# A decoder trunk on one core: column sums of the second norm spread among large products, a hand-made engine order through the up projection's fourth pair, two weight splits moved

## The chip, the cores and the metric

The kernel runs on one core of a Trainium2 chip. The metric is the device time of one execution in microseconds (us), of which three were taken before the change: 944.78, 944.92 and 948.59, median 944.92. In the text PE is the matrix engine and PEld its weight loads, DVE the vector engine, ACT the scalar engine, POOL the GpSimd engine, SP the queue that issues the DMAs. A time such as 271.10 is counted from the start of the profiled span.

## What is computed

One decoder layer of 1024 tokens and width 1024: a sliding-window attention, then a squared-ReLU MLP of 4096 hidden units, each behind an RMS norm, and a final norm.

```
u = rms_norm(h, attn_norm);  h = h + swa_mixer(u, w_qkv, sinks, w_o)
u = rms_norm(h, mlp_norm)
a = relu(u @ w_up);          h = h + (a * a) @ w_down
out = rms_norm(h, final_norm)
```

The change touches the second norm (that ahead of the MLP), and the first four of the sixteen groups of the up projection.

## The kernel before

Everything is held transposed: feature rows on the 128 partitions, tokens along the free axis, in two halves `hf` of 512 tokens. A float32 product is made of three fast products: each operand is split into a high part (a cast on ACT) and the low rest (a subtraction on DVE), and `mm3` or `mm3b` add high·high, high·low and low·high into one PSUM bank. One such matmul of 128 x 512 is called a large matmul here, and a product of the up projection is 12 of them.

**The second norm.** The second half of the attention's output projection makes 16 blocks, `oblock(m, hf)`: eight feature blocks m for tokens 0 to 511, then eight for the rest, 12 large matmuls each. Behind each block `oadd` adds it to the residual `h[m]` on DVE, and `square` squares it on ACT into a tile `sq2_m_hf`. Squares 1 to 5 are added onto square 0, one to four on POOL and the fifth on DVE; squares 6 and 7 stay apart. So three tiles hold what is left to sum, and `stat_sum` does it on PE with a vector of ones: `colsum` issues four matmuls with one output column for each tile, 12 in one row. Each is float32 and shows as two matmul records. Then come the root (`rstd`, ACT and small DVE operations) and a diagonal tile `dg` (`diag`, DVE), and `stat_bcast` multiplies it with ones (`n2b` in the trace), which brings the scale of each token to all partitions. `first_half` and `second_half` scale with it.

For tokens 0 to 511 the row of 12 stands behind block (0, 1), and `stat_bcast` behind block (1, 1). For the others the row stands behind the ninth matmul of the up projection's first product, and `stat_bcast` behind the ninth of its second.

**The up projection.** It is Strassen's: `up_mms(n, p)` is product n (1 to 7) of group p (0 to 15), and `up_evac` reads its bank. Products 1, 6, 7, 4 of a group accumulate in one bank of tag X (the copy out behind each must be done before the next may accumulate), product 2 uses Z, 5 and 3 one bank of Y. X has three banks, Y two, Z one. `c11`, `c22`, `c21` and `c12` are its four results, and seven stores per group go to a buffer in DRAM (`hid`). The weight combinations of a group are made from two loads of 512 KB (`wup[p, 0]`, `wup[p, 1]`) with four POOL operations, `up_sums`, and then split. In the rows `sa` and `sb` are the sums, `ws`, `wb`, `wt` and `wa` their splits (`_h`, `_l`).

**What sets the order.** PE always runs in the order in which the code issues (`pe.ordered`). From the second half of the output projection on, DVE, ACT and POOL do so too (`e.ordered = True`), until behind product (6, 2), where it is switched off. Where it is off, a scheduler sets the order of each engine when the kernel is built; each engine then runs its list strictly in that order, and waits at an instruction whose inputs are not ready. SP is one such list too.

Of the kernel before, what the change touches and what calls it, by code (L numbers as in the profile page):

```python
# [10 lines left out]
ALU = mybir.AluOpType  # L11
# [3 lines left out]
P = 128  # L15
# [7 lines left out]
NG = DFF // (2 * P)  # L23
# [39 lines left out]
def trunk(tc, xT, gains, wqkv, wo, wup, wdn, bias_d, sinks_d, ident_d, mask_d, outT):  # L63
# [73 lines left out]
    def colsum(ps, sq, n, first, last):  # L137
        for b in range(n):
            mm(ps[:, b:b + 1], sq[:, b * P:(b + 1) * P], ones[:, 0:1], first and b == 0, last and b == n - 1,
               skip_group_check=True)  # L140

    def rstd(ps, n, name):
        st = const.tile([P, 4, NB], F32, tag="st", name=f"{name}_st", bufs=3)
        var, y0, b_, y = (st[:, i, 0:n] for i in range(4))
        s.activation(y, ps[:, 0:n], AF.Sqrt, bias=eps, scale=1.0 / DM)
        v.tensor_scalar(var, ps[:, 0:n], 1.0 / DM, EPS, op0=ALU.mult, op1=ALU.add)
        v.reciprocal(y0, y)
        v.tensor_tensor(b_, y0, y0, op=ALU.mult)
# [453 lines left out]
    def split1(src, alloc, name):  # L602

        t = two(alloc(F32R, name))
        s.copy(t[:, 0], src)
        v.tensor_tensor(t[:, 1], src, t[:, 0].bitcast(F32), op=ALU.subtract)
        return t[:, 0], t[:, 1]

    def split2(src, alloc, name):

        hi, lo = two(alloc(F32R, f"{name}_h")), two(alloc(F32R, f"{name}_l"))
        s.copy(hi, src)
        v.tensor_tensor(lo, src, hi.bitcast(F32), op=ALU.subtract)
        return [(hi[:, i], lo[:, i]) for i in range(2)]
# [11 lines left out]
    hid = [[dram.tile([P, 2, 512], F32, name=f"hid{i}_{gg}") for gg in range(NG // 2)] for i in range(7)]  # L626
    stat = {}

    def stat_sum(hf):
        ps = bank("Y", f"n2s{hf}")  # L630
        parts = stat.pop(("sq", hf))
        for i, sq in enumerate(parts):
            colsum(ps, sq, 4, i == 0, i == len(parts) - 1)
        rn2 = rstd(ps, 4, f"n2_{hf}")
        dg = sqtile(f"dg2_{hf}")
        diag(rn2, 0, 4, dg)
        stat["dg", hf] = dg
# [6 lines left out]
    def square(m, hf):  # L644
        sl = HALVES[hf]
        sq = sqtile(f"sq2_{m}_{hf}")
        s.activation(sq, h[m][:, sl], AF.Square)
        parts = stat.setdefault(("sq", hf), [])
        if m in (0, 6, 7):
            parts.append(sq)  # L650
        else:
            (g if m < 5 else v).tensor_tensor(parts[0], parts[0], sq, op=ALU.add)

    x1, x2, XP = [], [], {}
    def scaled(out, i, hf, rb):
# [45 lines left out]
    def b22_split(i):  # L701
        XP["b22", i] = split1(h[2 * i + 1][:, HALVES[1]], atile if i else ktile, f"xc{i}")
# [65 lines left out]
    def up_mms(n, p, hooks={}):  # L768
        wn, xn = TERM[n]
        key = {1: "X", 6: "X", 7: "X", 4: "X", 2: "Z", 5: "Y", 3: "Y"}[n]  # L770
        first, last = n in (1, 2, 5), n in (4, 2, 3)
        if first:
            PS[key, p] = bank("mm" if n == 1 and p == 3 else key, f"u{key}{p}")
        for i in range(4):
            mm3b(PS[key, p], WU[wn, p], XP[xn, i], i, first and i == 0, last and i == 3)
            if i in hooks:
                hooks[i]()
# [15 lines left out]
    def c11_relu(p):  # L793
        c11 = OUT["a", p][:, 0]
        s.activation(c11, c11, AF.Relu)
        s.activation(c11, c11, AF.Square)
        store(2, p, c11)
# [64 lines left out]
    def oblock(m, hf):  # L862
        ps = bank(obanks[(hf * KT + m) % 5], f"o1_{m}_{hf}")
        for kk in range(4):
            mm3(ps, wsl(ws[m // 2], (m % 2) * 4 + kk), o_t[4 + kk], HALVES[hf], kk == 0, kk == 3)
        return ps
# [8 lines left out]
        e.ordered = True  # L875
    rb = None
    for m in range(KT):
        ps = oblock(m, 1)
        if m == 1:
            rb = stat_bcast(0)  # L880
        if 2 <= m < 5:
            LO[m - 1] = first_half(m - 1, rb)
        if 2 <= m < 6:
            XP["b11", m - 2], XP["b21", m - 2] = LO[m - 2]()
        if m == 6:
            WU["s2", 0], WU["s1", 0] = LO["ws0"]()
# [91 lines left out]
    for p in (2, 3):
        c11_relu(p)
    WU["a22", 2] = split1(u2[1][:, 1], walloc, "wb2")  # L980
    WU["s3", 2], WU["s4", 2] = split2(u2[0], walloc, "wt2")
    EARLY = 4
    order = [(7, 0), (7, 1), (4, 0), (3, 0), (5, 2), (4, 1), (6, 3), (3, 1), (7, 2), (5, 3), (4, 2), (3, 2),
             (7, 3), (1, 4), (4, 3), (2, 4), (3, 3)]
    for p in range(EARLY, NG):
        nxt = p + 1
        order += [(6, p), (5, p), (7, p)]
        order += ([(1, nxt)] if nxt < NG else []) + [(4, p)] + ([(2, nxt)] if nxt < NG else []) + [(3, p)]
    ready = 3
    for n, p in order:  # L990
        if (n, p) == (7, 1) or (n == 6 and p >= EARLY - 1):

            while ready <= min(max(p + 1, 3), NG - 1):
                raw = up_first(ready, walloc) if ready >= EARLY else None
                up_sums(ready, raw, temp)
                up_splits(ready)
                ready += 1
# [182 lines left out]
```

## Time and profile before

| | |
|---|---|
| median of three runs | 944.92 us |
| the profiled execution | 945.41 us |
| its span, first to last instruction | 943.7 us |
| PE in the chain that ended last | 88% of the span |
| PE waiting between 397 and 625 us | 0.7 us, once |
| mean granted clock of PE | 0.987 |

The chain of work that ended last is PE for 88% of the span. From 397 us to the end of the up projection PE waits once, for 0.7 us. So its waits lie in the first stage, around the second norm, in the first four groups of the up projection and in the final norm. PE's matmul records overlap (a 512-column one shows about 390 ns, while the next starts 226 ns later), so the distance of two starts is what counts.

### The profile page before, as it was taken

The numbers are of one execution on the slowest core, as the hardware profiler recorded it, in microseconds if no ns is written. First come the engines' busy times: TensorE is split into PE (matmuls) and PEld (weight loads), VectorE is DVE, ScalarE is ACT, GpSimd is POOL, SyncE is SP. The second block draws the span as 40 slices with busy tenths as digits, with TensorE's granted clock in tenths as the row PEclk, the third lists the DMA queues.
The fourth block names the chain that finished last, engine by engine and source line by source line (L and its number), as shares of the span: only waits on it lengthen the run. The fifth ranks groups of instructions, "written<-read, shape, count | busy, mean of one in ns | idle before, by whom it ended". The sixth has DMA issues, their size and how long they took to land.

```text
span 943.7 us, 12589 instructions
## 1 busy us (share of the span) xinstructions
PE 917.3 (97%) x4500; PEld 769.9 (82%) x4500; DVE 689.2 (73%) x952; ACT 445.7 (47%) x846; POOL 297.2 (31%) x258
## 2 busy tenths in 40 slices
PE   7999999999989998999999999999999999999996
PEld 6778888888878776888888888878888888888995
DVE  6779988999838886766575656565968785567964
ACT  8578878877534363433433333333333333445510
POOL 5116656566365015455435544110000000040200
PEclk9999999999999999999999999999999999999998
DMA  8200100501353024543454334799898988347622
GB/s 306 69 23 28 52 29 13 201 29 46 119 173 133 33 82 175 189 168 135 144 170 165 134 135 170 273 314 367 302 350 313 351 305 321 109 157 270 264 90 89
DMA packets 57325, 160.35 MB, mean 170 GB/s; under 512 B 6448, under 2 KB 10288, under 8 KB 57264
## 3 DMA queue, kind: packets, MB, share of 16 engines
q1 hardware_dynamic: 57264, 159.57, 47.6%
q8 instruction: 35, 0.57, 0.3%
q14 instruction: 26, 0.21, 0.1%
HBM read 121.79 MB, written 37.75 MB: 169 GB/s over the span
## 4 chain that ended last, share of the span: by engine, by line
PE 88%; DVE 6%; ACT 2%; issue 2%; DMA 1%; POOL 1%; SPq 0%; DVEq 0%; ACTq 0%
PE d L41 33%; PE uX L41 16%; PE f L41 12%; PE uY L41 9%; PE o L41 5%; PE uZ L41 4%; PE pv L41 3%; PE S L41 3%; PE pt L41 1%; DVE xl L41 1%; DMA xr<-xT 1%; PE n2s L41 1%; DVE oa L41 1%; DMA hid<-od 1%; DVE t L41 1%
## 5 line engine op out<-in xcount | busy, mean ns | idle before, releaser
L41 PE MATMUL d<-dx_h,dw_h 128*128 128x512 f32 (+1 forms) x512 | 186.5, 364 | 1.0 <-DVE hr L41 1.0
L41 PE MATMUL d<-dx_l,dw_h 128*128 128x512 f32 (+1 forms) x512 | 185.6, 362 | 0.0
L41 PE MATMUL d<-dx_h,dw_l 128*128 128x512 f32 (+1 forms) x512 | 185.6, 362 | 0.0
L41 PEld LDWEIGHTS d<-dx_h,dw_h 128*128 128x128 f32 x512 | 96.6, 189 | 16.5 <-DVE hr L41 1.4
L41 PEld LDWEIGHTS d<-dx_l,dw_h 128*128 128x128 f32 x512 | 96.6, 189 | 15.4 <-issue 0.2
L41 PEld LDWEIGHTS d<-dx_h,dw_l 128*128 128x128 f32 x512 | 96.6, 189 | 15.0
L41 ACT CAST dx_h<-hr 128x1024 fp32r<-128x1024 f32 x56 | 58.5, 1051 | 57.3 <-DVE dx_l L41 22.3
L41 DVE TENSOR_TENSOR dx_l<-hr,dx_h 128x1024 fp32r<-128x1024 f32 x56 | 71.6, 1285 | 17.6 <-ACT dx_h L41 17.5
L41 ACT CAST dw_h<-wf 128x1024 fp32r<-128x1024 f32 x40 | 41.9, 1052 | 89.6 <-PE d L41 70.7
L41 POOL TENSOR_TENSOR ssq3a<-ssq3a,sq_a 128x512 f32<-128x512 f32 x7 | 12.5, 1789 | 211.1 <-ACT sq_a L41 210.8
L41 DVE TENSOR_TENSOR dw_l<-wf,dw_h 128x1024 fp32r<-128x1024 f32 x40 | 48.6, 1220 | 28.1 <-ACT dw_h L41 27.9
L41 POOL TENSOR_TENSOR t<-t,sm 128x512 f32<-128x512 f32 x32 | 33.3, 1042 | 102.8 <-DVE sm L41 102.8
L41 DVE TENSOR_TENSOR wf<-wd,we 128x1024 f32<-128x1024 f32 x40 | 49.6, 1247 | 18.2 <-DMA we<-wdn 11.2
L41 ACT ACTIVATE t<-t,sm 128x129 f32<-128x129 f32 x128 | 50.5, 397 | 10.9 <-DVE sm L41 10.4
L41 PE MATMUL f<-xh,w_h 128*128 128x512 f32 x128 | 53.7, 420 | 0.0
L41 PE MATMUL f<-xl,w_h 128*128 128x512 f32 x128 | 50.9, 397 | 0.0
L41 PE MATMUL f<-xh,w_l 128*128 128x512 f32 x128 | 50.7, 396 | 0.0
L41 POOL TENSOR_TENSOR ob<-ob,oa 128x512 f32<-128x512 f32 x16 | 20.7, 1291 | 78.4 <-DVE ob L41 78.4
L41 PE MATMUL uX<-xu_h,wb 128*128 128x512 f32 x128 | 42.3, 391 | 2.4 <-ACT oa L41 2.4
L41 POOL TENSOR_TENSOR oc<-oc,oa 128x512 f32<-128x512 f32 x16 | 21.0, 1315 | 73.8 <-DVE oc L41 73.8
L41 ACT COPY oa<-uX 128x512 f32<-128x512 f32 x32 | 18.7, 587 | 49.9 <-PE uX L41 49.9
L41 POOL TENSOR_SCALAR_AFFINE_SELECT cur<-hl 128x1024 fp32r<-128x1024 f32 x32 | 39.5, 1235 | 2.0 <-DVE hl L41 2.0
(351 smaller groups left out, 2406.4 us busy)
## 6 DMA issues: line engine op xcount, KB each, us to landing
wd<-wdn SPq DMA_DIRECT2D x56, 512.0 KB, 5.7
hr<-hid SPq DMA_DIRECT2D x56, 512.0 KB, 4.8
we<-wdn SPq DMA_DIRECT2D x40, 512.0 KB, 7.0
hid<-oa SPq DMA_DIRECT2D x32, 256.0 KB, 2.4
hid<-oc SPq DMA_DIRECT2D x32, 256.0 KB, 2.3
hid<-ob SPq DMA_DIRECT2D x32, 256.0 KB, 2.5
w_r<-wqkv SPq DMA_DIRECT2D x8, 512.0 KB, 3.7
h<-xT SPq DMA_DIRECT2D x8, 512.0 KB, 6.3
```

The costliest lines, as they stand in the source:

```text
L41: ins = method(*args, **kw)
```

## The change

Three things are moved; the arithmetic is the same.

1. *Column sums.* `stat_part` no longer issues the one-column matmuls in a row, but puts them in a list `tiny`, and `mm` issues one behind each large matmul while the list holds any. Those of tokens 0 to 511 go among the 12 matmuls of block (0, 1), the first behind its first matmul; those of tile 0 of the other tokens go among the first four matmuls of block (7, 1), and the other eight among the first eight of the up projection's first product. All five additions of squares are on POOL now.
2. *Splits.* The two splits `a22` of groups 0 and 1 (`wb` in the rows) go from ahead of the loops to behind blocks (3, 1) and (4, 1); the loads of group 2 (`u2`) move from behind block (0, 1) to behind block (4, 1).
3. *Order by hand.* The switch to the scheduler's order comes later, behind product (7, 3). Ahead of it the work of groups 2 and 3 is written out, with `c22_sum` and `d1_sum` for parts of `up_evac`. PE's products are in another order too: (4, 1) is ahead of (5, 2), (3, 1) and (7, 2) ahead of (6, 3), and (4, 2) ahead of (5, 3).

```diff
     def mm(out, lhsT, rhs, start, stop, **kw):
         pe.matmul(out, lhsT=lhsT, rhs=rhs, start=start, stop=stop, **kw)
+        if tiny:
+            tiny.pop(0)()
...
+    def stat_part(hf, i, n=3):
+
+        if i == 0:
+            stat["ps", hf] = bank("Y", f"n2s{hf}")
+        ps, sq = stat["ps", hf], stat["sq", hf][i]
+        for b in range(4):
+            tiny.append(lambda b=b: pe.matmul(
+                ps[:, b:b + 1], lhsT=sq[:, b * P:(b + 1) * P], rhs=ones[:, 0:1], start=i == 0 and b == 0,
+                stop=i == n - 1 and b == 3, skip_group_check=True))
+
     def stat_sum(hf):
-        ps = bank("Y", f"n2s{hf}")
-        parts = stat.pop(("sq", hf))
-        for i, sq in enumerate(parts):
-            colsum(ps, sq, 4, i == 0, i == len(parts) - 1)
-        rn2 = rstd(ps, 4, f"n2_{hf}")
+        while tiny:
+            tiny.pop(0)()
+        rn2 = rstd(stat["ps", hf], 4, f"n2_{hf}")
...
-            (g if m < 5 else v).tensor_tensor(parts[0], parts[0], sq, op=ALU.add)
+            g.tensor_tensor(parts[0], parts[0], sq, op=ALU.add)
...
-    for p in range(2):
-        WU["a22", p] = split1(SUM[p][0][:, 1], wtile, f"wb{p}")
...
     for m in range(KT):
+        if m == 0:
+            for i in range(3):
+                stat_part(0, i)
+        if m == 7:
+            stat_part(1, 0)
         ps = oblock(m, 1)
...
-            u2 = up_load(2)
         if m == 1:
             LO[0] = first_half(0, rb)
+        if m in (3, 4):
+            WU["a22", m - 3] = split1(SUM[m - 3][0][:, 1], wtile, f"wb{m - 3}")
+        if m == 4:
+            u2 = up_load(2)
...
+    stat_part(1, 1)
+    stat_part(1, 2)
+    LO["wt0"] = his(SUM[0][2], wtile, "wt0")
     WU["s3", 0], WU["s4", 0] = LO["wt0"]()
-    up_mms(1, 0, {2: lambda: stat_sum(1)})
+    up_mms(1, 0)
+    stat_sum(1)
...
     up_product(6, 2)
     LO["wt1"] = his(SUM[1][2], otile, "wt1")
+    WU["a22", 2] = split1(u2[1][:, 1], walloc, "wb2")
     WU["s3", 1], WU["s4", 1] = LO["wt1"]()
+    c11_add(3)
+    u3 = up_load(3)
+    for i in range(3):
+        b22_split(i)
...
+    up_mms(7, 0)
+    c22_sum(0)
+    b22_split(3)
...
+    up_mms(7, 1)
+    c22_sum(1)
...
+    up_product(4, 0)
+    up_product(3, 0)
...
+    up_product(4, 1)
+    up_mms(5, 2)
+    up_product(3, 1)
...
+    up_product(7, 3)
     for e in (v, s, g):
         e.ordered = False
-    for i in range(4):
-        b22_split(i)
...
-    order = [(7, 0), (7, 1), (4, 0), (3, 0), (5, 2), (4, 1), (6, 3), (3, 1), (7, 2), (5, 3), (4, 2), (3, 2),
-             (7, 3), (1, 4), (4, 3), (2, 4), (3, 3)]
+    order = [(4, 3), (2, EARLY), (3, 3)]
```

What this makes of the engines' lists is shown at three places. The first is POOL ahead of block (0, 1). In the rows `sq_m_hf` is the square of feature block m and half hf, and `sb`, `sa` from `wu1b` and `wu1c` are the weight sums of group 1. Before, the list has no fifth addition:

```order
L41 TENSOR_TENSOR sq_0_0_3019<-sq_0_0_3019,sq_4_0_3086 128x512
L41 TENSOR_TENSOR sb_2994<-wu1c,wu1b 128x512
L41 TENSOR_TENSOR sa_2993<-wu1b 128x512
L41 TENSOR_TENSOR sa_2993<-wu1b,sb_2994 128x512
L41 TENSOR_TENSOR sb_2994<-wu1c,sa_2993 128x512
```

With the change POOL has:

```order
L41 TENSOR_TENSOR sq_0_0_3013<-sq_0_0_3013,sq_4_0_3080 128x512
L41 TENSOR_TENSOR sb_2994<-wu1c,wu1b 128x512
L41 TENSOR_TENSOR sa_2993<-wu1b 128x512
L41 TENSOR_TENSOR sa_2993<-wu1b,sb_2994 128x512
L41 TENSOR_TENSOR sq_0_0_3013<-sq_0_0_3013,sq_5_0_3097 128x512
L41 TENSOR_TENSOR sb_2994<-wu1c,sa_2993 128x512
```

The addition of square 5, which DVE made before, stands behind three weight sums of group 1. This piece is still in the part that the scheduler orders.

The second place is DVE in the second half of the output projection. `h_2046`, `h_2048` and `h_2050` are the residual adds of blocks 3, 4 and 5, `x_3` the scaled first half, `xb_l` its low parts, `wb` the moved splits. Before:

```order
L41 TENSOR_TENSOR h_2046<-o_3_1_3241,h_2046 128x512
L41 SCALAR_TENSOR_TENSOR x_3_3280<-h_2052,gn,n2b_3203 128x512
L41 SCALAR_TENSOR_TENSOR x_3_3280<-h_2054,gn,n2b_3203 128x512
L41 TENSOR_TENSOR xb_l<-x_2_3254,xb_h 128x1024
L41 TENSOR_TENSOR h_2048<-o_4_1_3267,h_2048 128x512
L41 TENSOR_TENSOR xb_l<-x_3_3280,xb_h 128x1024
L41 TENSOR_TENSOR h_2050<-o_5_1_3291,h_2050 128x512
```

With the change DVE has there:

```order
L41 TENSOR_TENSOR h_2046<-o_3_1_3231,h_2046 128x512
L41 TENSOR_TENSOR wb_3255<-wu0b,wb_3255 128x512
L41 SCALAR_TENSOR_TENSOR x_3_3273<-h_2052,gn,n2b_3193 128x512
L41 SCALAR_TENSOR_TENSOR x_3_3273<-h_2054,gn,n2b_3193 128x512
L41 TENSOR_TENSOR xb_l<-x_2_3244,xb_h 128x1024
L41 TENSOR_TENSOR h_2048<-o_4_1_3260,h_2048 128x512
L41 TENSOR_TENSOR wb_3284<-wu1b,wb_3284 128x512
L41 TENSOR_TENSOR xb_l<-x_3_3273,xb_h 128x1024
L41 TENSOR_TENSOR h_2050<-o_5_1_3291,h_2050 128x512
```

Each `wb` subtraction stands directly behind a residual add. On ACT, with the change, the cast that it needs stands behind the square of that same add:

```order
L41 ACTIVATE sq_3_1_3252<-h_2046 128x512
L41 CAST wb_3255<-wu0b 128x512
L41 CAST xb_h<-x_3_3273 128x1024
L41 ACTIVATE sq_4_1_3281<-h_2048 128x512
L41 CAST wb_3284<-wu1b 128x512
L41 ACTIVATE sq_5_1_3306<-h_2050 128x512
```

So the subtraction waits for the add, its square and its cast in turn.

The third place is DVE ahead of product (7, 1). `wt_l<-sb_2994` are the low parts that (7, 1) reads, `wb<-wu2b` the split for group 2, `xc` the split inputs of products 3, and `oa<-uY` the evacuation of (7, 0). Before:

```order
L41 TENSOR_TENSOR xc_3650<-h_2042,xc_3650 128x512
L41 TENSOR_TENSOR wt_l<-sb_2994,wt_h 128x1024
L41 TENSOR_TENSOR oa_3515<-uZ_3520,oa_3515 128x512
L41 TENSOR_TENSOR xc_3653<-h_2046,xc_3653 128x512
L41 TENSOR_TENSOR wb_3668<-wu2b,wb_3668 128x512
```

With the change:

```order
L41 TENSOR_TENSOR wb_3645<-wu2b,wb_3645 128x512
L41 TENSOR_TENSOR wt_l<-sb_2994,wt_h 128x1024
L41 TENSOR_TENSOR oa_3515<-uZ_3520,oa_3515 128x512
L41 TENSOR_TENSOR xc_3654<-h_2042,xc_3654 128x512
L41 TENSOR_TENSOR xc_3657<-h_2046,xc_3657 128x512
L41 TENSOR_TENSOR xc_3660<-h_2050,xc_3660 128x512
L41 TENSOR_TENSOR oa_3396<-uY_3566,oa_3396 128x512
```

The split of group 2 stands ahead of the low parts that (7, 1) needs now; its cast on ACT stands behind theirs.

More of the change, by code (lines that the diff above doesn't have):

```diff
@@ L107, in trunk @@
     v.memset(eps, EPS)
+    tiny = []
     def mm(out, lhsT, rhs, start, stop, **kw):
         pe.matmul(out, lhsT=lhsT, rhs=rhs, start=start, stop=stop, **kw)
+        if tiny:
+            tiny.pop(0)()
     def tr(out, in_):
@@ L893, in trunk @@
             nc.sync.dma_start(wu3, wup[3, 0])
-            u2 = up_load(2)
         if m == 1:
             LO[0] = first_half(0, rb)
+        if m in (3, 4):
+            WU["a22", m - 3] = split1(SUM[m - 3][0][:, 1], wtile, f"wb{m - 3}")
+        if m == 4:
+            u2 = up_load(2)
         if m == 5:
             LO["ws0"] = his(SUM[0][1], wtile, "ws0")
-        if m == 6:
-            LO["wt0"] = his(SUM[0][2], wtile, "wt0")
         if m % 2 == 1:
@@ L970, in trunk, with c22_sum, d1_sum @@
     LO["wt1"] = his(SUM[1][2], otile, "wt1")
+    WU["a22", 2] = split1(u2[1][:, 1], walloc, "wb2")
     WU["s3", 1], WU["s4", 1] = LO["wt1"]()
-    c11_relu(1)
-    c11_add(3)
+    c11_add(3)
+    u3 = up_load(3)
+    for i in range(3):
+        b22_split(i)
+    def c22_sum(p):
+        c22 = OUT["a", p][:, 1]
+        OUT["d", p] = temp(f"od{p}")
+        s.copy(c22, PS["X", p])
+        v.tensor_tensor(c22, PS["Y", p], c22, op=ALU.add)
+        relu2(c22, c22)
+        store(5, p, c22)
+    def d1_sum(p):
+        c11, c22 = OUT["a", p][:, 0], OUT["a", p][:, 1]
+        v.tensor_tensor(OUT["d", p][:, 0], c11, c22, op=ALU.add)
+        store(1, p, OUT["d", p][:, 0])
+    up_mms(7, 0)
+    c22_sum(0)
+    b22_split(3)
+    c11_relu(1)
+    LO["wt2"] = his(u2[0], walloc, "wt2")
+    d1_sum(0)
+    up_mms(7, 1)
+    c22_sum(1)
+    WU["s3", 2], WU["s4", 2] = LO["wt2"]()
+    s2_3 = up_sums_inplace(3, *u3)
+    d1_sum(1)
+    up_product(4, 0)
+    up_product(3, 0)
+    c11_relu(2)
+    up_product(4, 1)
+    up_mms(5, 2)
+    up_product(3, 1)
+    c11_relu(3)
+    WU["s2", 3] = split1(s2_3, walloc, "ws3a")
+    WU["s1", 3] = split1(u3[1][:, 0], walloc, "ws3b")
+    WU["a22", 3] = split1(u3[1][:, 1], walloc, "wb3")
+    up_product(7, 2)
+    WU["s3", 3], WU["s4", 3] = split2(u3[0], walloc, "wt3")
+    up_product(6, 3)
+    up_product(4, 2)
+    EARLY = 4
+    raw4 = up_first(EARLY, walloc)
+    up_mms(5, 3)
+    up_product(3, 2)
+    up_sums(EARLY, raw4, temp)
+    up_product(7, 3)
     for e in (v, s, g):
         e.ordered = False
-    for i in range(4):
-        b22_split(i)
[L978 to L982, printed above, removed]
-    order = [(7, 0), (7, 1), (4, 0), (3, 0), (5, 2), (4, 1), (6, 3), (3, 1), (7, 2), (5, 3), (4, 2), (3, 2),
-             (7, 3), (1, 4), (4, 3), (2, 4), (3, 3)]
+    up_product(1, EARLY)
+    up_splits(EARLY)
+    order = [(4, 3), (2, EARLY), (3, 3)]
     for p in range(EARLY, NG):
@@ L988, in trunk @@
         order += ([(1, nxt)] if nxt < NG else []) + [(4, p)] + ([(2, nxt)] if nxt < NG else []) + [(3, p)]
-    ready = 3
     for n, p in order:
[L991 to L997, printed above, removed]
+        if n == 6 and p + 1 < NG:
+            up_sums(p + 1, up_first(p + 1, walloc), temp)
+            up_splits(p + 1)
         up_product(n, p)
```

## The prediction, made before the changed kernel ran

> **What bounds the kernel now.** I began with the page. PE is busy for nearly the whole span:
>
> ```profile
> span 943.7 us, 12589 instructions
> PE 917.3 (97%) x4500; PEld 769.9 (82%) x4500; DVE 689.2 (73%) x952; ACT 445.7 (47%) x846; POOL 297.2 (31%) x258
> ```
>
> So the time changes only by what PE waits, by what it runs slowly, and by its own work. Next I read the waits of PE (total, times, longest), which name the places that the change aims at:
>
> ```profile
> PE uY L41 <- DVE ob L41: 4.4, 2, 2.9
> PE n2b L41 <- DVE dg L41: 2.6, 1, 2.6
> PE uX L41 <- ACT oa L41: 2.4, 2, 1.8
> ```
>
> PE waits 2.6 us for the diagonal of the second norm, 1.8 for a copy out behind product (7, 0), and 1.5 and 2.9 ahead of products (5, 2) and (5, 3). A wait has a second price, the clock, which the busy times by stretch show (PE, PEld, DVE, ACT, POOL busy, then the granted clock):
>
> ```profile
> 278.20:281.60 3.40, 1.24 (x6) 0.69 (x4) 1.99 (x6) 1.14 (x2) 0.14 (x1) 1.00 0.59 163
> 281.61:285.02 3.41, 2.98 (x5) 1.75 (x6) 1.84 (x4) 0.63 (x1) 1.27 (x1) 0.50 1.06 286
> 302.09:305.50 3.41, 3.41 (x29) 3.26 (x28) 1.81 (x2) 2.10 (x3) 3.41 (x3) 1.00 0.40 154
> 305.51:308.91 3.40, 3.40 (x10) 2.66 (x10) 2.56 (x7) 1.78 (x3) 0.62 (x1) 0.50 0.00 0
> 346.47:349.87 3.40, 1.63 (x7) 1.05 (x6) 2.53 (x4) 3.40 (x7) 0.00 (x0) 1.00 0.70 183
> 373.77:377.18 3.41, 3.41 (x9) 2.63 (x10) 3.34 (x5) 0.00 (x0) 1.06 (x1) 0.50 0.41 129
> ```
>
> The clock is granted in stretches of 3.41 us. Behind one with PE busy for 1.24 us the next is at 0.50; behind one with 1.63 us it is not. The stretch from 302.09, with some 2.6 us of one-column matmuls, counts as idle too. A slow stretch costs up to 1.7 us.
>
> [...]
>
> **The unit prices.** PE's rows give them:
>
> ```profile
> 271.10 0.39 PE L41 MATMUL o<-oh,wo_h 128*128 128x512 f32 x1
> 273.59 0.39 PE L41 MATMUL o<-oh,wo_l 128*128 128x512 f32 x1
> 302.81 2.73 PE L41 MATMUL n2s<-ones,sq 128*128 128x1 f32 x24
> 305.40 0.69 PE L41 MATMUL uX<-xb_h,wa_h 128*128 128x512 f32 x1
> 309.81 1.02 PE L41 MATMUL n2b<-dg,ones 128*128 128x512 f32 x2
> 310.90 0.40 PE L41 MATMUL uZ<-xb_l,wa_h 128*128 128x512 f32 x1
> ```
>
> The first two are the first and the twelfth matmul of block (0, 1): (273.59 - 271.10) / 11 = 0.226 us each. Twelve column-sum matmuls in a row take 305.40 - 302.81 = 2.59 us, 0.216 each. `n2b` takes 310.90 - 0.23 - 309.81 = 0.86.
>
> **Spreading the sums.** No row shows a column sum between large matmuls. If both its weight loads hide behind a large one it costs nothing, if none does 0.216 us. I take 0.216, the row's own price, since its two loads and the next large one's must follow each other and one of the three is hidden in the row as well. So the 24 sums cost 5.2 us as before, and what spreading can save is the clock.
>
> [...]
>
> **Stall 1: POOL.** The first sum now stands behind the first matmul of block (0, 1) and needs the addition of square 5. That stands on POOL behind three sums of group 1's weights:
>
> ```profile
> 268.66 0.33 SPq L732 DMA_DIRECT2D wu1b<-wup  x1
> 273.24 1.28 POOL L41 TENSOR_TENSOR sb<-wu1c,wu1b 128x512 f32<-128x512 f32 x1 [3.37 <-DMA wu1b<-wup]
> 275.70 1.27 POOL L41 TENSOR_TENSOR sa<-wu1b,sb 128x512 f32<-128x512 f32 x1
> ```
>
> The load is issued when POOL has read the buffer that it overwrites, and POOL's list up to there is unchanged, so it lands at 273.2 again. The third sum ends at 276.97, square 5 another 1.25 later (such additions take 1.27 to 1.30 here), at 278.22. PE could issue the first column sum at 271.10 + 0.23 = 271.33; it waits **6.9 us**, with everything behind it. Two stretches (271.37 and 274.78) are idle, so 278.20 to 281.60 runs at half clock: 3.35 us there lose **1.7**. Block (0, 1) with its 12 sums ends at 278.25 + 11 x 0.226 + 12 x 0.216 + 1.7 = 285.0.
>
> **Behind it, the wait for `dg` stays.** The chain to the diagonal:
>
> ```profile
> 274.02 0.69 DVE L41 TENSOR_TENSOR h<-o,h 128x512 f32<-128x512 f32 x1 [2.03 <-PE o L41]
> 274.80 0.63 ACT L41 ACTIVATE sq<-h 128x512 f32<-128x512 f32 x1 [2.09 <-DVE h L41]
> 275.45 1.28 ACT L41 ACT_TABLE_LOAD   x1
> 276.74 0.26 ACT L41 ACTIVATE n_st<-n2s,eps 128x4 f32<-128x4 f32 x1
> 305.57 0.26 ACT L41 ACTIVATE n_st<-n2s,eps 128x4 f32<-128x4 f32 x1 [1.30 <-PE n2s L41]
> 306.74 0.69 DVE L41 TENSOR_TENSOR dg<-ident,n_st 128x512 f32<-128x512 f32 x1
> ```
>
> Before, block (0, 1) ended ahead of the 12 sums, and its add, square and table load (274.02 to 276.73) ran beside them. Now the block's last matmul is as late as the sums, at 284.55, and the three are bare: the add at 284.98 (0.43 behind that start, as from 273.59 to 274.02), the root 2.72 later at 287.70, the diagonal's end 1.86 behind that (305.57 to 307.43) at 289.56. PE has only block (1, 1) to cover it, until 285.0 + 2.72 = 287.7. It waits **1.9 us**. Taking the two `wb` splits out of that chain is thus nearly eaten up.
>
> **Stall 2: the moved splits.** From 290.46 PE runs blocks (2, 1) to (6, 1). Five blocks later, at 290.46 + 13.6 + 0.23 = 304.29, it meets the first sum of the other tokens, which needs square 5 of block (5, 1) added on POOL. DVE's way to that block is long already, without idle time from the first DVE row here to the last add:
>
> ```profile
> 284.16 2.73 DVE L41 SCALAR_TENSOR_TENSOR x<-h,gn,n2b 128x512 f32<-128x512 f32 x4 [1.57 <-PE n2b L41]
> 286.80 1.22 DVE L41 TENSOR_TENSOR xb_l<-x,xb_h 128x1024 fp32r<-128x1024 f32 x1
> 297.32 0.68 DVE L41 TENSOR_TENSOR h<-o,h 128x512 f32<-128x512 f32 x1
> 298.08 0.64 ACT L41 ACTIVATE sq<-h 128x512 f32<-128x512 f32 x1 [1.10 <-DVE h L41]
> 293.28 1.30 POOL L41 TENSOR_TENSOR sq<-sq,sq 128x512 f32<-128x512 f32 x1 [2.49 <-ACT sq L41]
> 293.70 1.96 DVE L41 TENSOR_TENSOR xb_l<-x,xb_h 128x1024 fp32r<-128x1024 f32 x1
> 345.38 0.60 ACT L41 CAST wb<-wu2b 128x512 fp32r<-128x512 f32 x1
> ```
>
> From the first scaling to the end of block 5's add are 298.00 - 284.16 = 13.84 us. Now two `wb` subtractions stand in it. Bare they add 0.6 each. But each stands directly behind a residual add and waits for that add's square (0.64) and its own cast (0.60), some 1.2 us in which DVE's queue stands still, and then runs beside POOL's addition of that square (the `xb_l` beside one, at 293.70, took 1.96, another 1.22). I put each at 2.35, together 4.7: the add of block 5 ends 18.5 us behind the first scaling (which is at 290.66), its square 0.7 and POOL's addition 1.4 later, at 311.4. PE waits 311.4 - 304.3 = **7.1 us** (3.6 with bare splits). One stretch (305.5) is idle and the next nearly, so the clock is half until 315.7: 4.3 us lose **2.2** (0.5 to 3.9, by where the stretches fall). The second diagonal is ready in time: eight sums end in the up projection's first product, 1.86 + some 0.2 us later `dg`, ahead of it 4 + 9 large matmuls, 2.9 us.
>
> PE then loses 6.9 + 1.7 + 1.9 + 7.1 + 2.2 = 19.8 us in this stage. Before: from 271.10 to 310.67 are 39.57 us, with 117 large matmuls (26.5), 24 sums (5.2) and two `n2b` (1.7), so 6.2 were lost. **Stage one: +13.6.**
>
> **The order by hand.** Here the change does what PE's waits call for. These rows count:
>
> ```profile
> 334.58 0.62 ACT L41 CAST ws_h<-s 128x512 fp32r<-128x512 f32 x1
> 342.85 1.05 ACT L41 CAST wt_h<-sb 128x1024 fp32r<-128x1024 f32 x1
> 343.94 1.23 DVE L41 TENSOR_TENSOR wt_l<-sb,wt_h 128x1024 fp32r<-128x1024 f32 x1 [1.59 <-ACT wt_h L41]
> 345.34 0.39 PE L41 MATMUL uX<-xu_h,wt_l 128*128 128x512 f32 x1
> 351.47 3.05 DVE L41 SCALAR_TENSOR_TENSOR oa<-oa 128x512 f32<-128x512 f32 x2
> 373.63 0.69 PE L41 MATMUL uY<-xt_h,ws_h 128*128 128x512 f32 x1 [2.85 <-DVE ob L41]
> 397.14 0.39 PE L41 MATMUL uX<-xt_h,ws_h 128*128 128x512 f32 x1
> ```
>
> From 310.67 to the first matmul of (6, 4) at 397.14 are 86.47 us; 28 products and 3 matmuls, 339 x 0.2267, are 76.85. So 9.6 were lost: the three waits with restarts and one slow stretch, and 0.8 for `xt_l` ahead of (6, 0), which stays, as DVE's list up to there is the same. In the new order ACT copies (7, 0) out right behind four casts of 0.6, at some 346.5, while PE reaches (4, 0) only behind (7, 1), at 348.6. Two new waits come. (7, 1) reads `wt_l` at 345.34; DVE now has `wb` ahead of it, whose cast follows `wt_h` on ACT and ends at about 344.4; 0.7 for it and 1.23 for `wt_l` end at 346.3: 1.0. And (5, 2) needs the bank that the evacuation of (3, 0) frees; DVE runs beside POOL's four sums of group 3 there (two operations took 3.05 us there, while the `dg` one of that size took 0.69), which makes it late by about 1.5. Behind that each product finds its inputs by my reading. The later loads of group 2 cost nothing: released by the second `wb`, they land some 5 us later, about 311, with four POOL sums by 317, and the casts that read them stood at 334. 0.8 + 1.0 + 1.5 = 3.3 instead of 9.6: **-6.2**. Bounds: -8.8 with neither wait, -2 if DVE falls behind POOL twice as far.
>
> **The sum.** 13.6 - 6.2 = +7.4 on the profiled execution's 945.41: 952.8 us. That execution lies 0.5 above the median of 944.92, which is less than this can resolve.
>
> [...]
>
> **Rivals.** (a) *The column sums find their squares in time* and PE does not stop: that needs POOL to be through square 5 at 271.3 and 304.3. Then 19.8 shrinks to 1.9, and the time is 945.4 - 4.3 - 6.2 = 934.9, **faster**. It is decided by the load of `wu1b`: landing before 267.5 instead of 273.2. Against it: it is issued only at 268.66. (b) *Only stall 1 is gone*, by the same point: 952.8 - 8.6 = 944.2. (c) *Stall 2 is short*, since the splits cost their bare 0.6: 3.5 + 1.7 less, 947.6. For it: DVE's waits behind POOL may fall elsewhere. [...] (e) *The order by hand gives little*, or the clock stays half for one more stretch behind either stall: +2 to +5, about 956.
>
> **How the numbers follow.** The forecast 952.8 has 0.55, (d) 0.08, (e) 0.12, (c) 0.13, (b) 0.05, (a) 0.07. 0.5% (4.7 us, so 940.2 and 949.6) is about what a measurement of this kernel can tell from no change. Slower takes the forecast, (d) and (e), less 0.03 for their low ends: 0.72; same (c), (b) and that: 0.21; faster (a): 0.07. The range takes in (b) to (e) with the bounds of stall 2 and of the order by hand: 944.0 to 958.5; only (a) and the far ends are left out.
>
> **What would show it.** PE's waits should have two new rows, `n2s` for POOL `sq`, of about 7 us each; `n2b` for `dg` still about 1.9; the clock at 0.50 behind each of the two. POOL's addition of square 5 should start behind a sum of `wu1b` at about 277. In the order by hand the waits for `oa` and for `ob` ahead of (5, 3) should be gone, with 1.0 ahead of (7, 1). If no `n2s` wait shows, stage one is wrong and the time is below 945; if (6, 4) comes 10 us behind its sums, the second.

## The result, and the profile after

The change makes the kernel slower: median 960.45 us (959.43 to 962.46, four runs) against 945.21 of before beside it, ratio 1.0162, 95% interval 1.0146 to 1.0177. The forecast was 952.8, in a range from 944.0 to 958.5, so the sign was right and the size too small by half. The profiled execution took 962.46 us, 17.05 more than that of before.

The head of the page of the changed kernel, and its five largest waits of PE between 262 and 640 us (total, times, longest):

```profile
span 960.6 us, 12590 instructions
PE 924.1 (96%) x4500; PEld 774.9 (81%) x4500; DVE 690.9 (72%) x951; ACT 445.3 (46%) x847; POOL 303.1 (32%) x260
```

```profile
PE n2s L41 <- POOL sq L41: 13.5, 2, 6.8
PE uX L41 <- ACT ob L41: 1.9, 1, 1.9
PE uX L41 <- ACT oa L41: 1.8, 2, 1.1
PE uY L41 <- DVE ob L41: 1.5, 1, 1.5
PE uX L41 <- DVE wt_l L41: 0.8, 1, 0.8
```

The two new waits for POOL's squares are there, at their places and in their lengths (13.5 us for the 14.0 forecast). But PE is also busy for 6.8 us more than before, with the same 4500 instructions: it ran slowly. The busy times by stretch of 3.41 us (PE, PEld, DVE, ACT, POOL busy with their instructions, then the granted clock) show where:

```profile
271.29:274.70 3.41, 0.05 (x1) 0.00 (x0) 0.55 (x1) 0.63 (x1) 1.61 (x2) 1.00 0.57 209
274.71:278.11 3.40, 0.05 (x1) 0.05 (x1) 0.00 (x0) 0.00 (x0) 3.40 (x4) 0.50 0.00 0
278.12:281.53 3.41, 3.41 (x12) 3.12 (x13) 0.00 (x0) 0.00 (x0) 1.11 (x1) 0.50 0.35 100
281.54:284.94 3.40, 3.40 (x13) 3.01 (x13) 0.00 (x0) 0.00 (x0) 0.00 (x0) 0.50 0.55 209
284.95:288.35 3.40, 3.40 (x13) 3.02 (x13) 0.50 (x1) 0.00 (x0) 0.00 (x0) 0.50 0.00 1
288.36:291.76 3.40, 3.40 (x9) 2.63 (x9) 0.92 (x6) 2.17 (x3) 0.00 (x0) 0.50 0.20 77
291.77:295.17 3.40, 3.40 (x14) 2.21 (x14) 2.82 (x5) 0.63 (x1) 0.89 (x1) 1.00 0.20 77
308.84:312.24 3.40, 0.00 (x0) 0.00 (x0) 3.15 (x3) 0.13 (x1) 1.03 (x1) 1.00 0.35 108
312.25:315.65 3.40, 1.31 (x6) 1.21 (x6) 1.80 (x2) 1.56 (x2) 2.63 (x2) 0.50 0.44 172
315.66:319.07 3.41, 3.41 (x11) 2.93 (x12) 0.31 (x1) 0.63 (x1) 3.33 (x4) 0.50 0.22 82
319.08:322.48 3.40, 3.40 (x12) 2.73 (x11) 0.69 (x1) 0.55 (x2) 1.25 (x2) 0.50 0.00 0
322.49:325.89 3.40, 3.40 (x22) 3.06 (x23) 1.45 (x3) 1.53 (x4) 0.00 (x0) 1.00 0.20 77
```

Three stretches in a row, from 278.12 to 288.35, have PE busy all the time, and behind each the clock stays at 0.50. Behind 288.36, in which eight large matmuls start and no sum, it is at 1.00 again. PE's rows around the end of the first stall (start, duration) tell what it did meanwhile. The next row ends the second stall, and the last two are the first matmuls of (6, 4) and (7, 4):

```profile
270.95 0.39 PE L41 MATMUL o<-oh,wo_h 128*128 128x512 f32 x1
278.06 0.59 PE L41 MATMUL n2s<-ones,sq 128*128 128x1 f32 x2 [6.72 <-POOL sq L41]
278.51 0.77 PE L41 MATMUL o<-ol,wo_h 128*128 128x512 f32 x1
279.36 0.77 PE L41 MATMUL o<-oh,wo_l 128*128 128x512 f32 x1
...
314.34 0.59 PE L41 MATMUL n2s<-ones,sq 128*128 128x1 f32 x2 [6.79 <-POOL sq L41]
...
411.32 0.39 PE L41 MATMUL uX<-xt_h,ws_h 128*128 128x512 f32 x1
418.86 0.50 PE L41 MATMUL uX<-xu_h,wt_h 128*128 128x512 f32 x1 [1.94 <-ACT ob L41]
```

A large matmul comes every 0.85 us, with one sum between two of them: 0.43 for each at half clock. So a stretch holds four large matmuls.

**Where the 17.05 us come from.** Block (0, 1) starts at 270.95 and the second `n2b` ends at 329.11 (0.86 behind its start, as in the prediction): 58.2 us where before took 39.57, so +18.6. From there to the first matmul of (6, 4) at 411.32 are 82.2 us, before 86.47: -4.3. The wait of 1.94 behind it costs 2.1 with its restart. The rest, some 0.6, lies in the down projection and at the ends.

### The profile page after: what moved, and what is told of

Read it like the earlier page. It is cut to its first block, busy times and chain, and to the rows that moved or that the text cites. A ratio compares the mean times of both kernels' runs of the same rounds, so it can differ in the third digit from the quotient of the medians.

```text
span 960.6 us, 12590 instructions
## 1 busy us (share of the span) xinstructions
PE 924.1 (96%) x4500; PEld 774.9 (81%) x4500; DVE 690.9 (72%) x951; ACT 445.3 (46%) x847; POOL 303.1 (32%) x260
## 4 chain that ended last, share of the span: by engine, by line
PE 79%; DVE 8%; issue 4%; POOL 3%; ACT 3%; DMA 3%; SPq 0%; DVEq 0%; POOLq 0%; ACTq 0%
PE d L41 32%; PE uX L41 14%; PE f L41 12%; PE uY L41 7%; PE uZ L41 4%; PE pv L41 3%; PE S L41 3%; PE o L41 2%; PE pt L41 1%; POOL sa L41 1%; POOL sb L41 1%; DVE xl L41 1%; DMA wu0b<-wup 1%; DMA xr<-xT 1%; DMA wd<-wdn 1%
## 5 line engine op out<-in xcount | busy, mean ns | idle before, releaser
L41 POOL TENSOR_TENSOR ob<-ob,oa 128x512 f32<-128x512 f32 x16 | 24.2, 1511 | 80.3 <-DVE ob L41 80.3
```

The costliest lines, as they stand in the source:

```text
L41: ins = method(*args, **kw)
```

## Experiments

Two theories stood against each other for stage one. `ob`, like `oa`, is a copy out of a bank, and `xt_h`, `xt_l` are the split inputs of products 6 and 5. **Mine**, drawn from the rows above: a stretch is granted full clock only if the one before held enough large matmuls (eight did, four did not); with a sum behind each at half clock there are never enough, so a stall ahead of spread sums is paid twice. **Rivals:** spread sums draw the clock down by themselves; or a stall of this length costs a fixed number of slow stretches. The second rival meets a counterexample in the changed kernel itself: its two stalls are equally long (6.72 and 6.79 us), but five slow stretches go with the first and three with the second, behind which the rest of the block holds four sums and not twelve. All ratios are to before, measured beside it, with 95% intervals.

**1. Each part alone or undone.** First the fifth addition of squares on DVE again, all else as changed:

```diff
-            g.tensor_tensor(parts[0], parts[0], sq, op=ALU.add)
+            (g if m < 5 else v).tensor_tensor(parts[0], parts[0], sq, op=ALU.add)
```

> The changed kernel with the addition of the fifth squares back on DVE. Theory (the POOL list makes stall 1, and the clock behind it makes most of its price): stall 1 of 6.7 us and the 13.6 us at half clock behind it (6.8 lost) go; the wait for dg ahead of n2b comes back with about 2 us, stall 2 shrinks only by about 0.6 us to some 6.2. So 10 to 13 us less than the changed kernel: about 948 to 951, still slower than before. Rival A (one-column sums between large matmuls draw the half clock by themselves): the stall goes, but block (0, 1) still shows sums 0.57 us behind the large matmul, and only 6 to 8 us are gained: about 953. Rival B (the load of wu1b, not the addition, is what PE waits for): stall 1 stays in another place and the time hardly moves, about 960.

Measured: 949.01 us, ratio 1.0036 (1.0024 to 1.0049), 1.2% below the changed kernel for this one line. PE's rows in block (0, 1):

```profile
270.67 0.39 PE L41 MATMUL o<-oh,wo_h 128*128 128x512 f32 x1
270.90 0.28 PE L41 MATMUL n2s<-ones,sq 128*128 128x1 f32 x2
271.04 0.48 PE L41 MATMUL o<-ol,wo_h 128*128 128x512 f32 x1
271.35 0.28 PE L41 MATMUL n2s<-ones,sq 128*128 128x1 f32 x2
271.49 0.47 PE L41 MATMUL o<-oh,wo_l 128*128 128x512 f32 x1
```

Stall 1 is gone and a large matmul comes every 0.45 us; the clock stays at 1.00 there. So rivals A and B fall. 0.45 is 0.226 for each: a spread sum costs here its full price of a row (0.216), none of it hidden. `n2b` waits for `dg` again, 1.7 us, and stall 2 is still 6.2 us, with three slow stretches.

Then the first part undone (sums in rows, fifth addition on DVE; parts two and three kept):

```diff
-    def stat_part(hf, i, n=3):
...
-    up_mms(1, 0)
-    stat_sum(1)
+    up_mms(1, 0, {2: lambda: stat_sum(1)})
```

> The changed kernel with its first part undone: the sums in rows behind block (0, 1) and behind the ninth matmul of the first product, fifth squares added on DVE; the moved wb splits and the order by hand stay. Theory: no stall 1, no wait for dg (no splits in its chain), so full clock until the second row; that row waits some 2 to 5 us for squares that the moved wb splits made late, with one stretch at half clock behind it; order by hand worth 2.0 us as the changed kernel's trace shows it (4.2 up to product (6, 4), 2.2 given back behind it). About 943 (940 to 946). Rival (the moved splits are the bigger loss, whatever the sums): 950 or more. Rival (order by hand worth the 6.2 of the prediction): about 938.

Measured: 946.78 us, ratio 1.0014 (1.0004 to 1.0024). Above the range of the theory: the row waits 1.7 and 1.6 us for two squares, as expected, but two stretches behind it are at half clock, not one. One more is slow behind the wait ahead of (7, 4), and one behind the first row, where PE does not wait: the stretch ahead of it, from 272.15, is filled with sums and holds five large matmuls. In the kernels below that spread the sums without a stall this one does not come.

Before with the first part alone:

```diff
-            (g if m < 5 else v).tensor_tensor(parts[0], parts[0], sq, op=ALU.add)
+            g.tensor_tensor(parts[0], parts[0], sq, op=ALU.add)
...
-    up_mms(1, 0, {2: lambda: stat_sum(1)})
+    stat_part(1, 1)
+    stat_part(1, 2)
+    up_mms(1, 0)
+    stat_sum(1)
```

> Before with the first part alone: sums spread, all five additions of squares on POOL; wb splits and the order of the fourth group as before. Theory: stall 1 of about 6.7 us and some 13.6 us at half clock behind it (6.8 lost) as in the changed kernel; the wait for dg stays at 2 to 3 us, since the wb splits stand in its chain again; stall 2 falls to some 2 to 3 us, the splits being out of DVE's way there; the 1.7 us of half clock behind the second row go. About 957 (953 to 961). Rival (stall 2 is POOL's doing, not the splits'): stall 2 stays near 6.8 and the time is 963 or more.

Measured: 958.51 us, ratio 1.0134 (1.0120 to 1.0147). Stall 1 is 6.3 us, with five slow stretches as in the changed kernel; stall 2 is 1.3. So stall 1 is the first part's doing, and most of stall 2 that of the moved splits.

Before with the third part alone (the diff is that of the order by hand above):

> Before with the third part alone, the order by hand. Theory from the changed kernel's trace: product (6, 4) starts some 4.2 us earlier than before, and the wait for the copy ob ahead of product (7, 4), 1.9 us, gives 2.2 of it back: about 943 (942 to 944.5). Rival (the prediction's figure holds and the late wait is a result of the other parts): about 939. Rival (no gain at all): 945.

Measured: 944.97 us, ratio 0.9993 (0.9980 to 1.0005): no gain that shows, just above the range of the theory and at the figure of its third rival. From the first half of the up projection on its waits are those of the changed kernel, but two stretches around the one ahead of (7, 4) differ:

```profile
397.68:401.08 3.40, 1.45 (x7) 1.05 (x6) 2.28 (x3) 3.00 (x4) 1.23 (x2) 1.00 0.38 108
401.09:404.49 3.40, 3.40 (x10) 2.62 (x9) 3.37 (x6) 0.21 (x1) 0.73 (x1) 0.50 0.88 265
```

Here the wait of 1.95 us falls into one stretch, and the next is at half: 1.7 us more. In the changed kernel the same wait is split over two and costs nothing more. So the third part, as the change has it, is worth 2 us or nearly nothing, by where the stretches fall. Seven of the kept traces have this wait, of 1.94 to 1.98 us, and five of them show the slow stretch behind it.

**2. What holds the clock down.** The changed kernel with the same late square, but the twelve sums in a row behind block (0, 1):

```diff
         if m == 0:
+            for i in range(3):
+                stat_part(0, i)
             stat_sum(0)
```

> The changed kernel, fifth squares still added on POOL, but the twelve sums of tokens 0 to 511 in a row behind block (0, 1) in place of one behind each of its matmuls. It tells whether sums between large matmuls hold the clock down. Theory (a stretch is granted full speed only if the one before streamed enough columns; a one-column sum takes as long as a large matmul at half clock and streams nothing, so a mixed stretch never counts as busy): PE waits some 4.3 us for the same square, the clock is half for about three stretches from there (sums in a row, then plain large matmuls, which bring it back), and 12 fewer sum-and-matmul pairs run at half clock: about 4 us less than the changed kernel, 956 to 957.5. Rival (the clock stays half for five stretches behind such a stall, whatever runs): half until about 295, no gain, 960 or more.

Measured: 955.51 us, ratio 1.0114 (1.0099 to 1.0129), some 4.5 us less than with spread sums and half a us below the range. The stretches behind its wait of 3.9 us:

```profile
272.64:276.04 3.40, 0.25 (x2) 0.00 (x0) 0.69 (x1) 0.00 (x0) 3.40 (x4) 1.00 0.00 0
276.05:279.46 3.41, 2.66 (x13) 2.66 (x13) 0.00 (x0) 1.91 (x2) 1.92 (x2) 0.50 0.07 17
279.47:282.87 3.40, 3.40 (x15) 3.28 (x15) 0.41 (x3) 0.26 (x1) 0.00 (x0) 0.50 0.97 331
282.88:286.28 3.40, 3.40 (x9) 2.64 (x8) 1.02 (x3) 0.00 (x0) 0.00 (x0) 0.50 0.10 36
286.29:289.69 3.40, 3.40 (x14) 2.44 (x13) 2.53 (x4) 1.03 (x2) 1.14 (x1) 1.00 0.20 77
```

Three slow stretches in place of five, and the block itself ran at full clock. The gain has two parts. The wait is 2.8 us shorter, since the block's other large matmuls run ahead of it and not behind it; and PE works at half clock from 276.80 to 286.29 in place of 278.06 to 291.77, which loses 4.7 us and not 6.9. So behind this stall spreading the sums was worse than leaving them in a row (960.45 against 955.51 us).

Then a kernel in which PE has no wait around the second norm. It is made from the third kernel of experiment 3, which has neither stall and a mended order by hand; each sum of tokens 512 to 1023 is issued three times, twice into columns that nobody reads:

```diff
+        def cols(b):
+            for c in ((b, b + 4, b + 8) if b < 3 else (b + 4, b + 8, b)) if hf else (b,):
+                col(b, c)
         for b in range(4):
-            tiny.append(lambda b=b: pe.matmul(
...
+            tiny.append(lambda b=b: cols(b))
```

> The kernel with both mended, with each of the twelve one-column sums of tokens 512 to 1023 issued three times, twice into columns that nobody reads. PE then has three of them behind each large matmul of the first product, without any wait. It tells whether the clock follows PE's busy time or the large matmuls. Theory (a stretch of 3.41 us with five large matmuls or fewer makes the next one half, however busy PE is; here one holds 3.41 / 0.87 = 3.9): 0.50 shows inside the first product, and the time is 24 x 0.216 = 5.2 for the added sums and another 4 to 9 for the clock above the kernel it is made from: 944 to 950. Rival (the clock halves behind idle time only): no 0.50 there, 939.5 to 941.

Measured: 945.14 us, ratio 0.9997 (0.9984 to 1.0010), some 9 us above the kernel it is made from. Four stretches at half clock without a wait ahead of them, behind one in which PE was busy from end to end at full clock:

```profile
296.25:299.65 3.40, 3.40 (x29) 3.24 (x28) 1.52 (x2) 1.95 (x3) 0.00 (x0) 1.00 0.40 154
299.66:303.06 3.40, 3.40 (x17) 3.21 (x16) 0.00 (x0) 0.00 (x0) 0.00 (x0) 0.50 0.00 0
303.07:306.48 3.41, 3.41 (x16) 3.22 (x16) 0.00 (x0) 0.00 (x0) 0.00 (x0) 0.50 0.00 0
306.49:309.89 3.40, 3.40 (x16) 3.21 (x16) 0.00 (x0) 0.00 (x0) 0.00 (x0) 0.50 0.00 0
309.90:313.30 3.40, 3.40 (x10) 2.72 (x11) 2.53 (x8) 2.72 (x5) 0.00 (x0) 0.50 0.00 0
```

Each middle row holds two large matmuls at half clock. So here the clock went with the large matmuls, not with PE's busy time (3.40 of 3.40 us in the row of 296.25, and 0.50 behind it). It also marks a limit of experiment 1: one sum to each large matmul left the clock at 1.00 there, three did not here.

**3. Without the stalls.** The changed kernel with the `wb` splits and group 2's loads and sums moved behind the split of `wa3`:

```diff
-        if m in (3, 4):
-            WU["a22", m - 3] = split1(SUM[m - 3][0][:, 1], wtile, f"wb{m - 3}")
-        if m == 4:
-            u2 = up_load(2)
...
     WU["a11", 3], WU["a12", 3] = LO["wa3"]()
+    for p in range(2):
+        WU["a22", p] = split1(SUM[p][0][:, 1], wtile, f"wb{p}")
+    u2 = up_load(2)
+    s2_2 = up_sums_inplace(2, *u2)
```

> The changed kernel with the two wb splits and the loads and sums of group 2 moved once more, from behind blocks (3, 1) and (4, 1) to behind the split of wa3, where DVE and ACT are idle. Theory (stall 2 is made of the splits in DVE's list, each with its wait for ACT and beside POOL): stall 2 falls from 6.8 to 1 to 2.5 us and the 10 us at half clock behind it go; stall 1 stays with its 17 us. About 951 (950 to 953). Rival (stall 2 is set by the squares' additions on POOL): stall 2 above 5, 958 or more. Rival (the loads of group 2, now later, hold up its splits): a new wait of PE ahead of product (6, 2) or (5, 2).

Measured: 954.51 us, ratio 1.0104 (1.0089 to 1.0118). Stall 2 falls to 2.2 us, as expected, with one slow stretch left behind it. The time is 3.5 above the forecast: besides that stretch, one slow one shows behind the wait ahead of (7, 4), and a new wait of 0.4 for `xt_h` ahead of (6, 0).

With this, the fifth addition of the first half on DVE, the second half's sums all in the first product, and the root ahead of block (0, 1)'s add:

```diff
+            (v if (m, hf) == (5, 0) else g).tensor_tensor(parts[0], parts[0], sq, op=ALU.add)
...
+        if m == 0:
+            stat_sum(0)
         oadd(m, 1, ps)
```

> The changed kernel's spread sums without its two stalls: the fifth square of tokens 0 to 511 added on DVE, the wb splits late as in the kernel with these alone moved, the other tokens' twelve sums all in the first product, and the root issued ahead of block (0, 1)'s add, so that the diagonal is ready for n2b. Theory (spread sums are good for the clock where their squares are ready): no n2s wait, no n2b wait over 0.5, no half clock between 262 and 330 us; about 12 us less than with the fifth addition on DVE alone: 936 to 940. Rival A (sums between large matmuls draw the half clock even at full speed): 0.50 shows in these stretches, 941 or more.

Measured: 942.04 us, ratio 0.9969 (0.9957 to 0.9981). No wait for `n2b` or for a square shows, and no slow stretch between 262 and 327 us: stage one does what the theory says, with the sums spread. The time is above the range for another reason, two slow stretches later, behind waits for `xt_h` and `xt_l` (1.1 and 0.8) and ahead of (7, 4). Rival A's figure came out, but not its 0.50.

This kernel with the order by hand mended at four places:

```diff
-    WU["a22", 2] = split1(u2[1][:, 1], walloc, "wb2")
     WU["s3", 1], WU["s4", 1] = LO["wt1"]()
+    WU["a22", 2] = split1(u2[1][:, 1], walloc, "wb2")
...
+    b22_split(0)
     up_mms(7, 0)
     c22_sum(0)
+    for i in range(1, 4):
+        b22_split(i)
...
+    up_product(3, 1)
     up_mms(5, 2)
-    up_product(3, 1)
...
+    up_sums(EARLY, raw4, temp)
     up_product(3, 2)
-    up_sums(EARLY, raw4, temp)
```

> The kernel with spread sums and no stalls, and the order by hand mended at four places: wb2 split behind wt1's, the copy behind product (7, 0) ahead of three b22 splits, product (3, 1) ahead of (5, 2), the weight sums of group 4 ahead of the evacuation of (3, 2). Theory (each of the four waits in the order by hand is a place in one engine's list): the waits for wt_l (0.8), for oa (1.1), for ob ahead of (5, 2) (1.5) and ahead of (7, 4) (1.9), with their restarts 6.2 us in all, go: 930 to 934. Rival (DVE is the bound there, and a wait mended comes back as another): 935 or more.

Measured: 935.12 us, ratio 0.9901 (0.9888 to 0.9913), faster than both kernels. The waits for `wt_l`, for both `ob` and for `oa` ahead of (4, 0) are gone, and so is every slow stretch from 262 us to the end of the up projection. The waits for `xt_h` and `xt_l` (1.1 and 0.8) stay, and a new one of 0.8 for `oa` stands ahead of (4, 1). The time is 1 above the range, at the lower bound of the rival, which was right in so far as one mended wait came back in part in another place.

Before with the mended order alone:

> Before with the order by hand alone, mended at the same four places. Theory (the order by hand is worth what its own four waits leave of it): the waits for wt_l, oa, ob ahead of (5, 2) and ob ahead of (7, 4) go, with their restarts 6.2 us, and with the last of them the half-clock stretch behind it (1.7): 6 to 8 less than with the order by hand alone, 937 to 939.5. Rival (each wait mended comes back in another place): 942 or more.

Measured: 939.92 us, ratio 0.9943 (0.9927 to 0.9960), just above the range, 5 us below the order by hand as it was changed. Here too PE waits 0.8 for `oa` ahead of (4, 1).

Next, from the kernel with both mended, the `wb` subtractions in an idle piece of DVE's list, ahead of `ws_l`, with their casts earlier on ACT, and ACT's copy behind (7, 1) ahead of two operations:

```diff
         if m == 5:
+            for p in range(2):
+                v.tensor_tensor(wb[p][:, 1], SUM[p][0][:, 1], wb[p][:, 0].bitcast(F32), op=ALU.subtract)
+            u2 = up_load(2)
```

> The kernel with both mended (no stalls, order by hand at four places), with the wb casts on ACT behind xb 3's and the wb subtractions in DVE's 1.7 us of idle time ahead of ws_l, the loads of group 2 behind them; and ACT's copy behind product (7, 1) ahead of two other operations. Theory: POOL's four sums of group 2 leave the stretch in which DVE is dense (310 to 317), so the wait for xt_h (1.1) ahead of product (6, 0) goes and that for xt_l falls to 0.6; the wait for oa ahead of (4, 1) (0.8) goes or falls below 0.3: 932 to 934. Rival (DVE is the bound through the whole stretch, wherever the splits stand): 934.5 to 936.

Measured: 937.74 us, ratio 0.9919 (0.9903 to 0.9936): above both ranges, no better than its parent. The wait for `xt_h` went, as expected, but the adds of blocks 6 and 7 came late and PE waited 0.78 us for a square among the spread sums:

```profile
295.79:299.19 3.40, 2.62 (x17) 2.14 (x17) 1.71 (x4) 2.17 (x3) 0.00 (x0) 1.00 0.77 253
299.20:302.61 3.41, 3.41 (x13) 3.03 (x13) 0.97 (x1) 0.13 (x1) 2.20 (x2) 0.50 0.21 82
302.62:306.02 3.40, 3.40 (x9) 2.47 (x8) 3.04 (x6) 1.55 (x3) 2.81 (x3) 0.50 0.00 0
```

0.78 us of waiting, 3.4 us of clock: with the sums spread, even this small wait left a stretch with only five large matmuls, and two slow ones behind it. So they went behind those adds:

> The kernel before it with the two wb subtractions, and the loads and sums of group 2, behind the adds of blocks (6, 1) and (7, 1), where DVE waits 1.7 us for ACT's cast of wt. Theory (the subtractions ahead of ws_l made the adds of blocks 6 and 7 late, so PE waited 0.78 for a square among the sums, and this small wait brought a stretch down to five large matmuls and 6.8 us of half clock): no n2s wait over 0.2, no 0.50 between 290 and 310, the wait for xt_h stays away or under 0.4; 4 to 5 less than that kernel: 932.5 to 934.5. Rival (POOL's sums of group 2, again in the stretch in which DVE is dense, bring the waits for xt_h back): 934.5 to 936, no better than the kernel with both mended.

Measured: 934.05 us, ratio 0.9869 (0.9851 to 0.9888), the fastest of all. No slow stretch from 262 us to the end of the up projection, and these waits of PE over 0.2 us between 262 and 640 us:

```profile
PE uX L41 <- ACT oa L41: 1.5, 2, 0.8
PE uX L41 <- DVE xt_l L41: 0.6, 1, 0.6
PE uX L41 <- DVE ws3a L41: 0.5, 1, 0.5
```

## Why the prediction was right in sign and wrong in size

**Stall 1 and stall 2: right.** 6.9 and 7.1 us were forecast, 6.72 and 6.79 measured, by the mechanisms named. POOL's and DVE's rows:

```profile
273.09 1.26 POOL L41 TENSOR_TENSOR sb<-wu1c,wu1b 128x512 f32<-128x512 f32 x1 [2.95 <-DMA wu1b<-wup]
276.75 1.26 POOL L41 TENSOR_TENSOR sq<-sq,sq 128x512 f32<-128x512 f32 x1
...
303.25 1.44 DVE L41 TENSOR_TENSOR wb<-wu0b,wb 128x512 fp32r<-128x512 f32 x1 [1.21 <-ACT wb L41]
309.00 1.42 DVE L41 TENSOR_TENSOR wb<-wu1b,wb 128x512 fp32r<-128x512 f32 x1 [1.26 <-ACT wb L41]
```

The addition of square 5 stands behind the sums of `wu1b`, and each `wb` subtraction costs DVE 1.2 us of waiting and 1.4 of work. The experiments confirm both: the addition on DVE ends stall 1, and the splits elsewhere cut stall 2 to 2.2 or 1.3. The way of stall 2 came out too: the add of block 5 ended 18.4 us behind the first scaling (293.73 to 312.16), 18.5 forecast.

**The clock behind the stalls: the step that failed.** The prediction put "3.35 us there lose 1.7" behind stall 1 and 2.2 behind stall 2. PE ran at half clock from 278.06 to 291.77 and from 314.34 to 322.49, which lost 6.9 and 4.1: 11.0 in place of 3.9. I took one slow stretch behind each idle one and assumed that a busy PE then gets its clock back. But I had read off the stretch from 302.09 of before that one-column matmuls do not count, and did not apply it to my own case: at half clock a sum and a large matmul take 0.43 each, so a stretch of the spread block holds 3.41 / 0.85 = 4 large ones, as many as that stretch did. Twelve such pairs kept themselves slow. The stretches also fell otherwise than forecast (the first went slow at 274.71 already), which cost nothing, since PE stood still. Rival (e) named one more slow stretch as a chance; it was three behind stall 1 and one behind stall 2.

**The wait for `dg`: wrong here, right beside it.** 1.9 us were forecast; none came, because block (1, 1), mostly at half clock, took 4.1 us in place of 2.7 (288.47 to 292.57), and the chain to the diagonal was 0.4 us shorter than forecast. The two together just cover it, which was luck. With stall 1 gone it showed, 1.7 us.

**The order by hand: -6.2 forecast, -2.2 measured.** Up to (6, 4) it gave 4.3. The waits for `xt_l` (0.6), for `wt_l` (0.83) and ahead of (5, 2) (1.48) came as forecast. That for `oa` ahead of (4, 0), said to be gone, took 1.1. ACT's rows:

```profile
366.00 0.62 ACT L41 CAST xc<-h 128x512 fp32r<-128x512 f32 x1 [2.57 <-DVE xc L41]
367.38 0.62 ACT L41 CAST xc<-h 128x512 fp32r<-128x512 f32 x1 [0.76 <-DVE xc L41]
367.91 0.58 ACT L41 COPY oa<-uX 128x512 f32<-128x512 f32 x1
...
416.76 1.04 ACT L41 CAST wt_h<-sb 128x1024 fp32r<-128x1024 f32 x1 [0.32 <-POOL sb L41]
417.71 0.61 ACT L41 CAST wb<-wu5b 128x512 fp32r<-128x512 f32 x1
418.23 0.58 ACT L41 COPY ob<-uX 128x512 f32<-128x512 f32 x1
```

I counted the casts ahead of the copy as 0.6 each in a row; each waits for DVE's subtraction of the one before. And "behind that each product finds its inputs by my reading" was wrong at (7, 4): the copy `ob` stands behind the casts of group 5's sums, which POOL finished late, since group 4's sums now stand behind an evacuation on POOL. The mended kernels removed both `ob` waits, the one for `wt_l` and that for `oa` ahead of (4, 0). That no slow stretch stands behind the wait ahead of (7, 4) in this trace is luck too; with one the order by hand would have given, by estimate, 2.2 - 1.7 = 0.5.

**The sum.** The clock is 7.1 more than forecast, `dg` 1.9 and the stalls 0.5 less; the order by hand is 4.0 short. With 0.6 elsewhere and some 0.4 of restarts that makes the 9.7 us between the forecast +7.4 and the measured +17.05.

**The other rivals.** (a), (b) and (c) are out by the two stalls. (d), sums at half price (24 x 0.108 us less), is out by the 0.45 us per pair at full clock: as much as a large matmul alone (0.226) and a sum in a row (0.216). No run shows a sum at 0.108 us.

## What to carry to other kernels

Work that PE did in small matmuls was no cover for the clock here (3.40 of 3.40 us busy, 0.50 behind it): count the large matmuls in a stretch, at the clock that it would have, before you spread small ones among them. Spread only what has its inputs ready; one operation in the wrong engine's list cost 1.2% here, and a wait of 0.78 us cost 3.4 more in clock. And an order by hand is right only if each engine's list is followed with its own waits: a row of casts is not four casts long if each waits for another engine (2.57 and 0.76 us here, for casts of 0.62).

## What the runs showed of the hardware that I had not expected

**The clock went with the large matmuls.** I counted those that start in each stretch of 3.41 us between 255 and 620 us, in all 14 traces, leaving out stretches with `n2b`. With five or fewer the next stretch was at half clock in 49 cases of 49, with six in 1 of 7, with seven or more in none (59 stretches of seven to nine). It was the same whether the stretch itself ran at full clock or at half (three stretches of four large matmuls from 278.12 to 288.35 in the changed kernel, PE busy throughout), and whether PE waited (1.45 of 3.40 us busy at 397.68 with the order by hand alone), or was busy with one-column sums to the end (3.40 of 3.40 us at 296.25 in the kernel with three sums). A large matmul takes 0.226 us at full clock, 15 to a stretch, so in these traces the bar lies, by estimate, at 6 / 15, about 40% of what a stretch can hold at full clock: eight at half clock were enough (288.36 in the changed kernel), four with a sum each were not. The kernel with three sums was forecast by this bar before it ran. Whether the chip counts matmuls, their columns or something that goes with them is not shown. Of the stretches left out, four held three to five large matmuls beside a whole or half `n2b`, and full clock followed; how much `n2b` counts was not tested. Both of the fastest kernels have a stretch of just six (from 297.15 and 297.28), so they pass close to the bar.

**A one-column float32 sum was paid in full among large matmuls**: 0.45 us for the pair at full clock (with the fifth addition on DVE) and 0.85 at half (in the changed kernel), twice the price of a large one alone in both (0.226 and 0.43).
